# Attention with 16 heads in a conformer block: where two partial softmax sums are exchanged, values reordered once through DRAM, transposes issued in pairs

## The chip, the cores and the metric

The kernel runs on one core of a Trainium2 chip. A core has a matrix engine (PE), three engines for elementwise work (VectorE or DVE, ScalarE or ACT, GpSimd or POOL) and SyncE (SP), whose queue issues most DMA transfers. Each engine works through its own instructions in order. Times are microseconds of one execution of the whole program. The kernel before takes 1745.57 us, the median of three runs from 1742.99 to 1748.04.

## The reference

One block over a sequence of 1024 tokens of width 1024, in f32. One projection feeds a gated convolution branch, the queries, keys and values of 16 heads of 64, and two gates. Attention of a head is a mixture of three dilated windows, each a softmax of its own, mixed by their log-sums; that is one softmax over the union of the keys with counts. Then the branches are merged through the gates and a gated feed-forward layer with a short convolution follows.

```python
DILATION_GROUPS = ((128, 1), (512, 4), (2048, 16))
z = h @ w_in
glu_in, q, k, v, gate_logits = split(z)
...
for window, dilation in DILATION_GROUPS:
    o_g, lse_g = dilated_window_attention(q, k, v, slopes, window, dilation)
mix = softmax(stack(lses), axis=0)
o = einsum('gbsh,gbshd->bshd', mix, stack(outs))
...
x = x + (g_a * y_a + g_b * y_b) @ w_out
x = x + ffn(rms_norm(x))
```

## The kernel before

Every f32 operand of a product is held as two parts, high and low, so that PE works in its fast f32 form; `split` (lines 87 and 88) makes them, the high part as a rounded copy, the low part as a subtraction on DVE or POOL. The stages by time in the profile: the gated linear unit and first gates up to 235 us; the projection to q, k and v up to 519.5; attention up to 910; the merge and the output projection up to 1130; the feed-forward layer to the end.

**The projection** runs over six blocks of 512 columns: block `ch` is of kind `ch % 3` (0 q, 1 k, 2 v) and of head group `ch // 3` (heads 0 to 7, 8 to 15). So blocks 0, 1, 2 are q, k, v of group 0, and 3, 4, 5 those of group 1. Within a block there are eight token tiles of 128. The weights come in four pieces of 512 KB each (`raw_qkv`, line 92), used first by the first tile. Results are normalised and transposed three tiles later (q and k: `qh`, `ql`, two buffers each) or only split (v), and then spilled to DRAM by SP (`spill`, line 154): `dq`, `dk`, and `dv` (512 KB per tile: 128 tokens x 8 heads x 128 values, the 128 being 64 high and 64 low).

**Attention** runs over heads, each in eight slots of 128 queries. The keys of a query fall in two sets: near ones (its own and the previous tile of 128) and those of the same class modulo 4. The near scores are computed for queries in natural order, the others for queries in order of their class (`order` makes that copy on POOL). So for each head there are 8 near rows-tiles and 8 class tiles with their own minima and sums, `st[:, 0]`, and to join both into one softmax each order needs the other's numbers. They go through DRAM: `exchange` (lines 825 to 831) writes both halves, 8 KB each, out to `dst` (lines 828 and 829), reads them back in the other order into `st[:, 1]` (830 and 831). All four are on SP, so the reads stand in its queue until the writes have landed, and what follows on SP stands behind them. `factor_first` (836, 837 on DVE, then an exponential on ACT in 838) and `factor_last` (843 to 846) make a factor per query row, `share` (856, POOL) multiplies the rows with it, `flip` (865, PE) transposes a slot's tiles of 128 into PSUM (`pp`), `split` makes `ph` on ACT and `pl` on DVE, and `weigh` (880, PE) adds them times the values into `o`.

The values must lie with the keys on the partitions, in both orders. `values` (line 778 on) fetches them per head from `dv` by six transfers: four for the class-ordered tile of near keys, two for the tile of the same class. `head` fetches q, kh, kl in halves (256 KB each) and the mask.

Order: in attention the instructions of ACT, DVE and PE keep the order in which the code is written; SP and POOL are ordered by a scheduler. One loop runs over slots `at`. Slot `n` of head `h` scores; in slot 0 `exchange` of the head before; in slot `MERGE` its factors; `BACK` delays the shares, transposes and weighing of the head before; `FILL` is the rate at which matmuls of other stages (gates and the convolution's output, `next(gates)`) are put in between:

```python
if n == 2 and h + 1 < H: tiles[h + 1] = head(h + 1)
if n == 5 and h + 1 < H: order(h + 1, 0)
if n == 0 and 0 < h <= H: exchange(h - 1)
if n == 5 and h < H: values(h)
first = n == MERGE and 0 < h <= H      # MERGE = 3
s0 = at - 7 - BACK                     # shares, BACK = 5
s1 = at - 8 - BACK                     # transposes, weighed a slot later
```

Of the kernel before, what the change touches and what calls it, by code (L numbers as in the profile page):

```python
# [21 lines left out]
P = 128  # L22
D = 1024
T = 1024
# [10 lines left out]
FILL = (2.8, 1.53, 2.0)  # L35
MERGE = 3
BACK = 5
# [23 lines left out]
def block_kernel(ctx: ExitStack, tc: tile.TileContext, x, xT, w_first, g1, g2, pack, mask,  # L61
# [100 lines left out]
    dv = [dr.tile([T, 8, P], F32R, name=f"dv{i}") for i in range(2)]  # L162
# [433 lines left out]
    with tc.tile_pool(name="ph1", bufs=1, reuse_waits="tile") as p1, ExitStack() as rest:  # L596
# [137 lines left out]

        tails = []
# [39 lines left out]
    with tc.tile_pool(name="ph2", bufs=1, reuse_waits="tile") as p2:  # L775
        vals, stats, rows, factors = {}, {}, {}, {}

        def values(h):
            near, same = (p2.tile([P, 8, P], F32R, tag=f"v{i}", bufs=2, name=f"v{i}_{h}") for i in range(2))
            src = dv[h // 8]  # L780
            for r in range(4):
                fetch(near[32 * r : 32 * r + 32], src.rearrange("(i j r) h e -> r j i h e", i=8, r=4)[r][:, :, h % 8, :])
            for b in range(2):
                fetch(same[:, 4 * b : 4 * b + 4, :],
                      src.rearrange("(b p r) h e -> b p r h e", b=2, r=4)[b][:, :, h % 8, :])
# [38 lines left out]
        def exchange(h):  # L824
            st = stats[h]
            far = lambda i: dstat[i][h].rearrange("(r j) (a f) -> (j a) r f", r=4, a=4)
            own = lambda i: st[:, i, 8:16, :].rearrange("p (r b) s -> p r (b s)", r=4)
            sp.dma_start(dstat[0][h], st[:, 0, 0:8, :])
            sp.dma_start(far(1), own(0))
            sp.dma_start(own(1), far(0))  # L830
            sp.dma_start(st[:, 1, 0:8, :], dstat[1][h])
# [9 lines left out]
        def factor_last(h, w):  # L841
# [7 lines left out]
        SHARES = [[(0, 0), (1, 0), (1, 4), (0, 1)], *([(1, i), (1, 4 + i), (0, 1 + i)] for i in (1, 2, 3)),  # L849
                  [(0, 5)], [(0, 6)], [(0, 7)]]  # L850
# [75 lines left out]
        with tc.manual_schedule(engines={ENG.Activation, ENG.DVE, ENG.PE}):  # L926
            pend = []
            for at in range(8 * H + 8 + BACK + 1):
# [17 lines left out]
                if s0 >= 0 and s0 % 8 < 7 and s0 // 8 < H:  # L946
# [622 lines left out]
```

## Time and profile before

| | |
|---|---|
| median of three runs | 1745.57 us |
| profiled execution, its own time | 1747.96 us |
| span of that execution, first to last instruction | 1746.1 us |
| mean granted clock of PE | 0.991 |
| PE busy in the span | 98% |
| DMA, mean over the span | 169 GB/s, 294.36 MB |

A line of the timeline reads: start, duration, engine, source line, operation, tiles written <- tiles read, partitions x elements, and in brackets the idle time ahead with what released it. A row of the waits has the time in all, the number and the longest. In a table of stretches each row is a stretch from A to B, with the busy time of each engine in it. The granted clock is the share of its full speed that PE was allowed. `SPq` is SP's queue, on which a transfer is issued; the landing is later. "Share" of DMA is the mean busy share of the core's 16 DMA engines.

### The profile page before, as it was taken

The page shows a single profiled execution, that of the slowest core. Times are in us where ns is not written, and L with a number is a line of the kernel's source. Part 1 is how long each engine was busy: PE and PEld are TensorE (multiplying, and loading weights), DVE is VectorE, ACT ScalarE, POOL GpSimd, SP SyncE. Part 2 cuts the span into 40 slices and gives each one's busy share as a digit, 9 for nine tenths or more (in the row PEclk, how much of TensorE's full clock was granted, in tenths as well). Part 3 has the DMA queues.
Part 4 walks back from the last instruction along what each step waited for, and adds up shares of the span by engine and source line. Part 5 has one row for each costly group of instructions (what it writes and reads, how often), then busy time and mean ns, then how long its engine had stood idle before and what let it go on. Part 6 is the DMA issues. An engine that isn't in the chain of part 4 may idle for free.

```text
span 1746.1 us, 23765 instructions
## 1 busy us (share of the span) xinstructions
PE 1709.8 (98%) x8384; PEld 1427.8 (82%) x8384; DVE 1272.5 (73%) x1926; ACT 838.6 (48%) x1482; POOL 517.3 (30%) x511
## 2 busy tenths in 40 slices
PE   9999999999998999989999999999999999999999
PEld 8888888887887788878888888888888888878877
DVE  6999999989743566766645564787767777879863
ACT  5543345554344566656645342555445445533431
POOL 0078749999503455665530000000000000000000
PEclk9999999999999999999999999999999999999999
DMA  8323264553468677787537585622222222499851
GB/s 318 121 98 108 77 231 139 153 179 118 128 242 218 149 196 186 213 219 189 147 114 270 196 308 208 224 98 84 85 85 74 95 85 73 150 331 326 284 175 48
DMA packets 189590, 294.36 MB, mean 169 GB/s; under 512 B 35104, under 2 KB 100896, under 8 KB 189216
## 3 DMA queue, kind: packets, MB, share of 16 engines
q1 hardware_dynamic: 187744, 289.70, 51.5%
q10 hardware_dynamic: 1728, 3.15, 0.5%
q8 instruction: 66, 1.08, 0.3%
q14 instruction: 52, 0.43, 0.1%
HBM read 212.84 MB, written 79.95 MB: 168 GB/s over the span
## 4 chain that ended last, share of the span: by engine, by line
PE 81%; DMA 11%; DVE 3%; issue 2%; ACT 1%; SPq 1%; POOL 1%; ACTq 0%; DVEq 0%; POOLq 0%
PE qkv L151 14%; PE xz L131 6%; PE xz L132 6%; PE xz L133 6%; PE wo L151 5%; PE dx L1394 5%; DMA dst<-st 5%; PE dy L1394 4%; PE glugv L355 3%; PE y L132 2%; PE y L131 2%; PE y L133 2%; PE uxz L133 2%; PE uxz L132 2%; PE uxz L131 2%; PE o L880 2%
## 5 line engine op out<-in xcount | busy, mean ns | idle before, releaser
L636 DVE SCALAR_TENSOR_TENSOR work<-apad,pk,work 128x1024 f32<-128x1024 f32 x188 | 241.5, 1284 | 3.4
L88 DVE TENSOR_TENSOR pl<-pp,ph 128x512 fp32r<-128x512 f32 (+2 forms) x128 | 77.7, 607 | 96.6 <-ACT ph L87 96.1
L856 POOL TENSOR_SCALAR p<-p,w 128x256 f32<-128x256 f32 (+1 forms) x256 | 111.6, 458 | 54.2 <-DVE w L846 41.5
L822 ACT ACTIVATE p<-p,st 128x256 f32<-128x256 f32 (+1 forms) x256 | 118.6, 466 | 16.9 <-DVE st L815 14.9
L151 PE MATMUL qkv<-hi_qkv,hT 128*128 128x512 f32 x384 | 115.0, 393 | 0.0
L1297 DVE SCALAR_TENSOR_TENSOR u<-u,pk 128x1023 f32<-128x1023 f32 x88 | 112.2, 1277 | 1.0 <-ACT u L1295 0.7
L815 DVE CUSTOM_DVE_ANT_0 p<-s,m 128x256 f32<-128x256 f32 (+1 forms) x256 | 87.0, 377 | 33.3 <-PE s L809 30.3
L627 POOL TENSOR_TENSOR part<-prod,part 128x1024 f32<-128x1024 f32 x43 | 103.5, 2407 | 21.3 <-ACT prod L626 16.8
L87 ACT ACTIVATE ph<-pp 128x512 fp32r<-128x512 f32 (+2 forms) x128 | 67.6, 528 | 76.0 <-PE pp L865 67.7
L880 PE MATMUL o<-ph,v 128*128 128x128 f32 (+1 forms) x336 | 84.7, 311 | 15.7 <-ACT ph L87 15.7
L151 PEld LDWEIGHTS qkv<-hi_qkv,hT 128*128 128x128 f32 x384 | 71.4, 188 | 14.7
L88 DVE TENSOR_TENSOR lo_uv<-raw_uv,hi_uv 128x1024 fp32r<-128x1024 f32 x20 | 24.5, 1226 | 79.8 <-ACT hi_uv L87 79.8
L880 PE MATMUL o<-pl,v 128*64 128x128 f32 (+1 forms) x336 | 77.5, 247 | 2.9 <-DVE pl L88 2.5
L151 PE MATMUL wo<-hi_wo,mT 128*128 128x512 f32 x256 | 80.1, 391 | 0.0
L865 PE MATMUL pp<-ident,p 128*128 128x128 f32 x432 | 74.0, 283 | 6.2 <-POOL p L856 5.5
L865 PEld LDWEIGHTS pp<-ident,p 128*128 128x128 f32 x432 | 56.8, 145 | 27.4 <-POOL p L856 11.6
L880 PEld LDWEIGHTS o<-ph,v 128*128 128x128 f32 x336 | 63.1, 198 | 18.3 <-ACT ph L87 18.3
L793 POOL CAST q<-q 128x512 fp32r<-128x512 f32 x32 | 36.0, 1128 | 132.1 <-DMA q<-dq 105.2
L131 PE MATMUL xz<-blk_t,hi_s3g 128*128 128x512 f32 x176 | 68.6, 390 | 0.7 <-ACT xc L1271 0.7
L131 PE MATMUL xz<-h2left,hi_uv 128*128 128x512 f32 x176 | 68.7, 390 | 0.0
L133 PE MATMUL xz<-h2left,lo_uv 128*128 128x512 f32 x176 | 68.5, 389 | 0.0
L132 PE MATMUL xz<-blk_t,hi_s3g 128*128 128x512 f32 x176 | 68.5, 389 | 0.0
(399 smaller groups left out, 5317.2 us busy)
## 6 DMA issues: line engine op xcount, KB each, us to landing
wr<-w_down SPq DMA_DIRECT2D x45, 512.0 KB, 5.6
gr<-dff SPq DMA_DIRECT2D x62, 256.0 KB, 5.1
raw_qkv<-w_qkv SPq DMA_DIRECT2D x24, 512.0 KB, 4.3
dff<-u SPq DMA_DIRECT2D x22, 512.0 KB, 2.6
raw_uv<-w_up SPq DMA_DIRECT2D x21, 512.0 KB, 3.2
raw_ug<-w_up SPq DMA_DIRECT2D x20, 512.0 KB, 3.2
q<-dq SPq DMA_DIRECT2D x32, 256.0 KB, 5.9
dv<-v SPq DMA_DIRECT2D x16, 512.0 KB, 2.8
```

The lines of the kernel that those rows point to most:

```text
L131: pe.matmul(o, wh[:, k, :], bh[:, k, :], start=(start and k == 0), stop=False, skip_group_check=not start)
L132: pe.matmul(o, wh[:, k, :], bl[:, k, :], start=False, stop=False, skip_group_check=not start)
L133: end = pe.matmul(o, wl[:, k, :], bh[:, k, :], start=False, stop=(k == 3), skip_group_check=not start)
L151: pe.matmul(ps, l, r[:, k % 2, :], start=(n == 1), stop=(n == 3 * KT))
L627: pool.tensor_tensor(out=a[:, CW - 1 :] if j == CW - 1 else part, in0=prods[j % 3], in1=part, op=ALU.add)
L636: dve.scalar_tensor_tensor(out=a[:, CW - 1 :] if j == CW - 1 else work, in0=a[:, j : j + T], scalar=w(c, j), in1=part if j == n else work, ...
L822: act.activation(pt, pt, AF.Exp, bias=st[:, 0, at, 0:1], scale=-1.0, accum_out=st[:, 0, at, 1:2])
L856: pool.tensor_scalar(pt, pt, f, 1.0, op0=ALU.mult, op1=ALU.mult)
L865: pe.transpose(o.rearrange("p (a j) -> p j a", a=4) if j < 2 - x else o, t, ident)
L880: pe.matmul(view(o[:m]), v[:, :m], t, start=(start and i == 0), stop=(stop and i == 0), skip_group_check=True)
L1297: dve.scalar_tensor_tensor(out=acc[:, d:], in0=src[:, : T - d], scalar=w(2 - d), in1=acc[:, d:], op0=ALU.mult, op1=ALU.add)
L1394: pe.matmul(banks[n], a[:, c], b[:, d], start=(start and i == 0 and m == 0), stop=(stop and i == nf - 1 and m == 2), skip_group_check=True)
```

## The change

What it does, part by part:

- Each group of values has three DRAM tiles: `dv[g][2]` takes the spill in natural order, and `sort_values(g, tt)` copies each 512 KB tile twice, from DRAM to DRAM, into `dv[g][0]` (the near order, sorted by class within 128 tokens) and `dv[g][1]` (the class order). For group 0 this stands behind each spill in block 2; for group 1 two tiles per head behind the exchange of heads 0 to 3, that is in slot 0 of heads 1 to 4.
- `values` fetches two contiguous-row tiles with two transfers instead of six, in slot 0 of the next head, behind the head's loads.
- `exchange` is split. `exchange_out` (two writes, SP) is issued in slot 0; the next head's loads, the values and the sort copies are issued after it. `exchange_in` (two reads) is on ACT's queue in slot `MERGE - 2 = 2`.
- `MERGE` goes from 3 to 4 and `BACK` from 5 to 7; `FILL` goes down slightly; `order(h + 1, 0)` stands in slot 6 instead of 5; the shares are laid out over eight slots.
- The transposes of two slots stand together in every second slot, and `weigh` of one slot is done in each slot ahead of them.

```diff
-FILL = (2.8, 1.53, 2.0)
-MERGE = 3
-BACK = 5
+FILL = (2.7, 1.48, 2.0)
+MERGE = 4
+BACK = 7
...
-    dv = [dr.tile([T, 8, P], F32R, name=f"dv{i}") for i in range(2)]
+    dv = [[dr.tile([T, 8, P], F32R, name=f"dv{i}_{a}") for a in range(3)] for i in range(2)]
...
-                spill(dv[g8][tt * P : (tt + 1) * P], vt.rearrange("p h s d -> p h (s d)"))
+                spill(dv[g8][2][tt * P : (tt + 1) * P], vt.rearrange("p h s d -> p h (s d)"))
+                if g8:
+                    to_sort.append((g8, tt))
+                else:
+                    sort_values(g8, tt)
...
+        def sort_values(g8, tt, by=sp):
+            src = dv[g8][2].rearrange("(i j r) h e -> i r j (h e)", i=8, r=4)[tt]
+            near = dv[g8][0].rearrange("(i r j) h e -> i r j (h e)", i=8, r=4)[tt]
+            same = dv[g8][1].rearrange("(b r a j) h e -> b a r j (h e)", b=2, r=4, a=4)[tt // 4, tt % 4]
+            for dst in (near, same):
+                by.dma_start(dst.bitcast(F32), src.bitcast(F32))
...
-            src = dv[h // 8]
-            for r in range(4):
-                fetch(near[32 * r : 32 * r + 32], src.rearrange("(i j r) h e -> r j i h e", i=8, r=4)[r][:, :, h % 8, :])
-            for b in range(2):
-                fetch(same[:, 4 * b : 4 * b + 4, :],
-                      src.rearrange("(b p r) h e -> b p r h e", b=2, r=4)[b][:, :, h % 8, :])
+            for t, src in zip((near, same), dv[h // 8]):
+                fetch(t, src.rearrange("(i p) h e -> p i h e", p=P)[:, :, h % 8, :])
...
-        def exchange(h):
+        def exchange_out(h):
...
             sp.dma_start(dstat[0][h], st[:, 0, 0:8, :])
-            sp.dma_start(far(1), own(0))
-            sp.dma_start(own(1), far(0))
-            sp.dma_start(st[:, 1, 0:8, :], dstat[1][h])
+            return sp.dma_start(far(h, 1), turned(st, 0))
+
+        def exchange_in(h):
+            st = stats[h]
+            act.dma_start(turned(st, 1), far(h, 0))
+            act.dma_start(st[:, 1, 0:8, :], dstat[1][h])
...
-                    if n == 2 and h + 1 < H:
-                        tiles[h + 1] = head(h + 1)
+                    if n == 0 and h == 0:
+                        tiles[1] = head(1)
...
-                    if n == 5 and h + 1 < H:
+                    if n == 6 and h + 1 < H:
                         order(h + 1, 0)
                 if n == 0 and 0 < h <= H:
-                    exchange(h - 1)
-                if n == 5 and h < H:
-                    values(h)
-                s0 = at - 7 - BACK
+                    with tc.issue_after(exchange_out(h - 1).ins):
+                        if h + 1 < H:
+                            tiles[h + 1] = head(h + 1)
+                        values(h - 1)
+                        for t in to_sort[2 * h - 2 : 2 * h]:
+                            sort_values(*t)
+                if n == MERGE - 2 and 0 < h <= H:
+                    exchange_in(h - 1)
+                s0 = at - 6 - BACK
...
-                flips = []
                 s1 = at - 8 - BACK
-                if 0 <= s1 < 8 * H:
-                    flips.append(flip(s1 // 8, s1 % 8))
-                for w in pend:
-                    done = weigh(*w) or done
-                pend = flips
+                if pend and s1 >= 1:
+                    done = weigh(*pend.pop(0))
+                if 0 <= s1 < 8 * H and s1 % 2 == 0:
+                    pend += [flip(s // 8, s % 8) for s in (s1, s1 + 1)]
```

SP's order at the end of block 2, before: the last spills of values (`dv`), the four weight pieces of block 4 (`raw_qkv`), the first spill of block 3 (`dq`).

```order
L154 DMA dv_82<-v_6_2798 128x1024
L92 DMA raw_qkv_0_3177<-w_qkv 128x1024
L154 DMA dv_82<-v_7_2827 128x1024
L92 DMA raw_qkv_1_3183<-w_qkv 128x1024
L92 DMA raw_qkv_2_3189<-w_qkv 128x1024
L92 DMA raw_qkv_3_3195<-w_qkv 128x1024
L154 DMA dq_0_76<-qh_0_2999 512x1x128
```

The same place after the change:

```order
L154 DMA dv_2_84<-v_6_2814 128x1024
L746 DMA dv_0_82<-dv_2_84 128x1x1024
L746 DMA dv_1_83<-dv_2_84 4x32x1024
L92 DMA raw_qkv_0_3197<-w_qkv 128x1024
L154 DMA dv_2_84<-v_7_2845 128x1024
L746 DMA dv_0_82<-dv_2_84 128x1x1024
L746 DMA dv_1_83<-dv_2_84 4x32x1024
L92 DMA raw_qkv_1_3203<-w_qkv 128x1024
L92 DMA raw_qkv_2_3209<-w_qkv 128x1024
L746 DMA dv_0_82<-dv_2_84 128x1x1024
L746 DMA dv_1_83<-dv_2_84 4x32x1024
L92 DMA raw_qkv_3_3215<-w_qkv 128x1024
```

Two copies (`L746`) per tile of values now stand between the spills and the weight pieces; the last piece stands behind all sixteen copies of group 0. The shape shown is the destination's; the source of both copies is the same, 4x32x1024 (four classes of 32 rows).

SP's order around the first exchange, before (`st` is the table of minima and sums of head 0, `q`, `kh`, `kl` the loads of head 2):

```order
L157 DMA q_4517<-dq_0_74 64x1024
L157 DMA kh_4518<-dk_0_78 64x1024
L828 DMA dst_0_84<-st_4270 128x16
L829 DMA dst_0_100<-st_4270 128x4x4
L157 DMA kl_4519<-dk_1_79 64x1024
L830 DMA st_4270<-dst_0_84 128x4x4
L831 DMA st_4270<-dst_0_100 128x16
L157 DMA q_4517<-dq_1_75 64x1024
```

And after the change:

```order
L838 DMA dst_0_88<-st_4301 128x16
L839 DMA dst_0_104<-st_4301 128x4x4
L157 DMA q_4486<-dq_0_74 64x1024
...
L736 DMA m_4489<-mask 128x512
L157 DMA v_0_4497<-dv_0_82 128x8x128
L157 DMA v_0_4498<-dv_1_83 128x8x128
L746 DMA dv_0_85<-dv_2_87 128x1x1024
L746 DMA dv_1_86<-dv_2_87 4x32x1024
L746 DMA dv_0_85<-dv_2_87 128x1x1024
L746 DMA dv_1_86<-dv_2_87 4x32x1024
L240 DMA dgate_128<-gs_1_4516 128x512
```

The writes of the exchange stand ahead of the loads, and the reads are gone from SP. ACT has them, two slots on, among the exponentials (`L831`) of head 1:

```order
L831 ACTIVATE p_1_1_4526,st_4474<-p_1_1_4526,st_4474 128x128
L843 DMA st_4301<-dst_0_88 128x4x4
L844 DMA st_4301<-dst_0_104 128x16
L831 ACTIVATE p_1_2_4551,st_4474<-p_1_2_4551,st_4474 128x256
L831 ACTIVATE p_1_2_4553,st_4474<-p_1_2_4553,st_4474 128x128
```

The exponentials of head 1's later slots stand behind the reads there.

More of the change, by code (lines that the diff above doesn't have):

```diff
@@ L822, in powers @@
             act.activation(pt, pt, AF.Exp, bias=st[:, 0, at, 0:1], scale=-1.0, accum_out=st[:, 0, at, 1:2])
-        def exchange(h):
+        far = lambda h, i: dstat[i][h].rearrange("(r j) (a f) -> (j a) r f", r=4, a=4)
+        turned = lambda st, i: st[:, i, 8:16, :].rearrange("p (r b) s -> p r (b s)", r=4)
+        def exchange_out(h):
             st = stats[h]
-            far = lambda i: dstat[i][h].rearrange("(r j) (a f) -> (j a) r f", r=4, a=4)
-            own = lambda i: st[:, i, 8:16, :].rearrange("p (r b) s -> p r (b s)", r=4)
             sp.dma_start(dstat[0][h], st[:, 0, 0:8, :])
-            sp.dma_start(far(1), own(0))
-            sp.dma_start(own(1), far(0))
-            sp.dma_start(st[:, 1, 0:8, :], dstat[1][h])
+            return sp.dma_start(far(h, 1), turned(st, 0))
[3 more added lines that the diff above has]
+            act.dma_start(st[:, 1, 0:8, :], dstat[1][h])
         def factor_first(h):
@@ L847, in factor_last @@
             factors[h] = w
-        SHARES = [[(0, 0), (1, 0), (1, 4), (0, 1)], *([(1, i), (1, 4 + i), (0, 1 + i)] for i in (1, 2, 3)),
-                  [(0, 5)], [(0, 6)], [(0, 7)]]
+        SHARES = [[(0, 0), (1, 0), (1, 4), (0, 1)], [(1, 1), (1, 5), (0, 2)], [(1, 2), (1, 6), (0, 3)],
+                  [(1, 3), (1, 7), (0, 4)], [(0, 5)], [(0, 6)], [(0, 7)], []]
         def share(h, i, n):
@@ L938, in block_kernel @@
                         order(h, 1)
[L939 removed]
+                    if n == 6 and h + 1 < H:
                         order(h + 1, 0)
                 if n == 0 and 0 < h <= H:
[L942 to L946 removed]
+                    with tc.issue_after(exchange_out(h - 1).ins):
[7 more added lines that the diff above has]
+                s0 = at - 6 - BACK
+                if 0 <= s0 < 8 * H:
                     for i, k in SHARES[s0 % 8]:
```

1 line of the change is left out of this document (added).

## The prediction

> **What bounds the kernel now.** I read the page's first part, then a table of stretches, then the waits, and last the chain with one stall in full.
>
> ```profile
> PE 1709.8 (98%) x8384; PEld 1427.8 (82%) x8384; DVE 1272.5 (73%) x1926; ACT 838.6 (48%) x1482; POOL 517.3 (30%) x511
> ...
> L151 PE MATMUL qkv<-hi_qkv,hT 128*128 128x512 f32 x384 | 115.0, 393 | 0.0
> ```
>
> The matrix engine (PE) is busy for 1709.8 of 1746.1 us. The change adds and removes no matmul and no transpose, so all that it can win is PE's 36 us of idle time and what PE loses to a lowered clock; all that it can lose is new idle time. The table of stretches says where both lie. Its columns are the stretch, its length, then busy time (and instructions) of PE, PE's weight loads, VectorE (DVE), ScalarE (ACT) and GpSimd (POOL), the granted clock, the DMA share and GB/s. The first row is the loading at the start, the second block 2 of the projection (the first value block) with most of block 3, the third the rest of the projection, and the last two are attention.
>
> ```profile
> 10.00:14.00 4.00, 4.00 (x18) 3.07 (x17) 3.04 (x4) 4.00 (x7) 0.00 (x0) 1.00 1.03 420
> 348.00:425.00 77.00, 75.25 (x344) 62.02 (x343) 71.22 (x72) 42.34 (x50) 72.18 (x33) 1.00 0.39 130
> 425.00:520.00 95.00, 95.00 (x454) 78.86 (x453) 65.66 (x78) 35.55 (x50) 35.49 (x20) 1.00 0.55 189
> 520.00:640.00 120.00, 111.51 (x671) 96.02 (x670) 59.45 (x237) 65.76 (x214) 51.13 (x84) 0.94 0.76 195
> 640.00:912.00 272.00, 255.65 (x1698) 221.83 (x1696) 165.65 (x580) 163.48 (x508) 149.38 (x246) 0.97 0.66 177
> ```
>
> In attention PE is idle for 8.5 us (120 less 111.51) and 16.4 us (272 less 255.65), 24.9 us together. The clock of 0.94 and 0.97 costs up to another 7.2 and 8.2 us (6% of 120, 3% of 272). In the projection PE has nothing to win: 75.25 of 77 us busy, then 95.00 of 95. Those 95 us are the last two of its six blocks, 47.5 us a block and 5.9 for each of the eight tiles of a block. The waits within attention (time in all, times, longest) say who holds PE up there:
>
> ```profile
> DVE w L836 <- DMA st<-dst: 28.9, 13, 4.7
> ACT w L838 <- DVE w L837: 47.9, 16, 5.2
> PE o L880 <- ACT ph L87: 15.7, 10, 3.5
> SPq L830 <- DMA dst<-st: 56.0, 15, 4.9
> PE pp L865 <- POOL p L856: 5.5, 4, 4.7
> ```
>
> DVE waits 28.9 us for the exchanged sums, 13 times in 16 heads. SyncE (SP), whose queue issues the transfers in order, itself stands 56.0 us for the outgoing write before it may issue the read. ACT stands behind it, and PE waits 15.7 us for the split of the transposes that ACT makes next. One of these stalls in the timeline (start, duration, engine, line, tiles), with the stretch of normal clock gone behind it:
>
> ```profile
> 744.90 0.55 SPq L828 DMA_DIRECT2D dst<-st  x1
> 751.77 0.38 SPq L830 DMA_DIRECT2D st<-dst  x1
> 755.57 0.82 DVE L836 TENSOR_TENSOR w<-st 128x16 f32<-128x16 f32 x1 [3.35 <-DMA st<-dst]
> 757.26 0.48 ACT L87 ACTIVATE ph<-pp 128x384 fp32r<-128x384 f32 x1
> 757.80 0.46 PE L880 MATMUL o<-ph,v 128*128 128x128 f32 x1 [3.48 <-ACT ph L87]
> 759.09 0.63 PE L123 MATMUL ya<-aT,hi_co 128*128 128x512 f32 x1
> ```
>
> The outgoing write is issued at 744.90, the read back at 751.77, DVE starts at 755.57 after 3.35 us of waiting, PE at 757.80 after 3.48. The gap is followed by a matmul of 0.63 us for 512 columns (the projection's row above has 393 ns for as many). So the attention stage is bounded by PE with an exchange of 8 KB that comes some 3 us late per head.
>
> **Part 1: the exchange, the pairs, the order of the slots.** The outgoing writes go ahead of the next head's loads, the read goes on ACT's queue two slots later, the factors are made one slot later, the transposes two slots later. In the chain the outgoing writes of successive heads read so:
>
> ```profile
> 548.71 5.47 DMA dst<-st
> 571.01 5.70 DMA dst<-st
> 637.32 6.39 DMA dst<-st
> 744.90 6.81 DMA dst<-st
> 752.25 3.24 DMA st<-dst
> ```
>
> Between 548.71 and 637.32 lie four heads: 22.15 us a head, 2.77 a slot. The moves give one slot for the factors (2.77), two for the transposes (5.54), and about 3.6 us of the write's 6.81 if it lands like the read (3.24) once no load stands ahead of it: near 12 us of room against a lateness of 3.5. So the stalls of the exchange go wherever the queue isn't otherwise fuller. For 640 to 912 that is at most 16.4 + 8.2 = 24.6 us. I take **-20**, since a few of these gaps are not of the exchange (PE's 15.7 us waiting for ACT is over the whole of attention, of 24.9 idle). The ends are -24.6 and 0, the latter if the wait only moves. Pairing the transposes removes no instruction and I cost it at nothing: PE works through gate matmuls meanwhile. If that cover fails, the price is PE's wait for POOL's scaled rows, 5.5 us over all of attention in the row above. Fetching the values with two issues instead of six moves the same 512-byte pieces; it frees SP of four issues a head, which were off PE's path. The wait that SP sheds (56.0 us, 15 times, 3.7 each) is now on ACT, and what stands behind it there are the exponentials of the running head, for which DVE, POOL and then PE wait. It is two slots behind the write, 5.5 us, so it is short if the write lands like the read.
>
> **Part 2: the sort copies.** New are 32 copies of 512 KB from DRAM to DRAM (line 746 of the changed kernel), 16 per group. The trace of before has no such operation. The bounds of one: all sixteen DMA engines at the 420 GB/s of the first row (share 1.03), 0.524 MB in **1.25 us**; or a single engine at a sixteenth of that, **20 us**. Where between them depends on how many engines one copy occupies. The order of instructions shows what is different: every transfer of before starts with a count of 32, 64, 128 or 512, every copy has a side that reads 4x32x1024, four runs of rows lying apart. I take four engines, one for each run: 105 GB/s, **5.0 us**, which is also the middle of the two ends by ratio. While it runs, those four engines serve nothing queued later, and a transfer that uses all sixteen ends when its share on the four does.
>
> The Trainium skill, DMA: Bandwidth & Descriptors, section "Why a DMA increments its semaphore by 16 and not by 1", states that a DMA uses the largest number of engines up to 16 that divides the slowest dimension above 1 of both its patterns. By it a copy with 4 outermost runs has four engines and the sum below stays as it is; without it, with sixteen engines, the sum would be that of the first rival. No run here shows it yet.
>
> *Projection.* Copies of group 0 stand behind each spill of block 2 on SP, and ahead of the weights of block 4 and of the first spills of block 3:
>
> ```profile
> 348.21 2.12 SPq L154 DMA_DIRECT2D dv<-v  x2
> 382.27 7.42 SPq L92 DMA_DIRECT2D raw_qkv<-w_qkv  x3
> 402.38 0.56 SPq L154 DMA_DIRECT2D dq<-qh  x1
> 377.69 1.04 ACT L87 ACTIVATE hi_qkv<-raw_qkv 128x1024 fp32r<-128x1024 f32 x1
> 424.39 1.41 PE L151 MATMUL qkv<-hi_qkv,hT 128*128 128x512 f32 x5
> ```
>
> From 348 on the four engines have the work of before, 0.39 of 77 us = 30 us, less about 5 for spills of block 3 that stand behind the weights, and 16 x 5.0 = 80 us of copies: the fourth weight piece lands at 348 + 25 + 80 = 453, and ACT's split of it ends at 454. PE starts block 4 at 424.39 and needs that piece some three quarters of a tile of 5.9 us later, 428.8. The first spill of block 3, issued at 402.38 before, is queued behind too; with two buffers the third tile's q waits for it, and PE's accumulators fill up at about the same time. PE stalls for 454 less 428.8, **+25**. Ends: +3 if nothing of the old work is in the way (348 + 2.8 for the first spill + 80), +73 if a copy takes 8 us; and no cost at 1.25 us, where 20 us of copies fit into the 0.61 that is free.
>
> *Attention.* Group 1 is copied in heads 1 to 4, two tiles (four copies, 20 us) per head. The old work on each engine there is 0.76 x 22.15 = 16.8 us a head, together 36.8 against 22.15. Four heads: 147 less 88.6 = 58.7 us late, of which the room of 12 us from part 1 is taken once: **+47**. Ends: +20, if the 0.76 holds waiting and only 195 of 420 GB/s is work (0.46 x 88.6 + 80 - 88.6 - 12); +94 for copies of 8 us. The exchange, the next head's loads and the values all stand in this queue. In these heads the stalls of before are inside the new ones, so part 1 wins nothing there.
>
> **Sum.** -20 + 25 + 47 = +52. The profiled execution took 1747.96 us (span 1746.1 and 1.9 around it); that gives 1800. The median of the runs, 1745.57, is 2.4 below it, so 1798 there; I say **1799**.
>
> **The rivals.**
>
> *Sixteen engines for a copy (faster).* The mechanism is the same queue with the price of 1.25 us: then 20 us of copies fit beside the projection's 0.39 and raise the 0.76 of heads 1 to 4 to 0.76 + 5/22.15 = 0.99, just within. All stalls of the exchange go, three quarters of the 24.9 + 15.4 us: -30, 1716. The point from which it decides is a copy of about 1.4 us in attention, and three to four us in the projection. For it speaks that every transfer of before reaches all engines; against it that none of those has so short a first count. Chance 0.13.
>
> *The wait only moves.* ACT's read lands no sooner than SP's, since both queues share the engines. Part 1 wins nothing: 25 + 47 = +72, 1818. Against it: the room of 12 us. Chance 0.06.
>
> *A copy costs 8 us,* because it reads and writes the same memory: 73 + 94 - 20 = +147, 1893; 20 us on one engine goes far beyond. Chance 0.06.
>
> *Only one stage pays,* since SP's own waits keep the copies from piling up, or the weights come early enough: 25 - 20 or 47 - 20, 1751 to 1773. Chance 0.11; a fifth of it within 0.3%.
>
> *The forecast:* 0.64.
>
> **How the numbers follow.** A measurement of this kernel can tell about 0.3% (5 us) from no change. Faster by more is the first rival alone, 0.13. Within 0.3%: 0.02 from the fourth. Slower: 0.85. The range reaches from 1755, where the fourth rival's larger half and the forecast's low ends lie (both low at once, 3 + 20 - 20, would be 1749), to 1880, just under the 8 us copies. It leaves out the first rival, about 0.05 above and a little below, some 0.2.
>
> **What would show it.** Right: a stretch from about 400 to 455 in which the DMA share falls toward 0.25 at some 100 GB/s, with PE idle for 20 to 30 us of it before block 4's first tile is through; copies that land long after 5 us because they queue for one another; head periods over 30 us for heads 1 to 5 and at or under 21.5 us later; from head 6 on no wait of DVE for st<-dst and a clock near 1.00. Wrong: PE at 95 us of 95 in the projection and periods of 22 us from the first head (then the copies are spread), or the wait of DVE for the exchange still there in late heads (then part 1 is wrong), or a bound that I do not name, such as ACT held by its own DMA's wait.

## The result and the profile after

The changed kernel takes 1837.12 us (median of 4 runs, 1828.01 to 1839.97) against 1744.99 for the kernel before (four runs as well): a ratio of 1.0517, 95% interval 1.0477 to 1.0557. It is slower by 5%, inside the range of 1755 to 1880 and well above the 1799 forecast. The profiled execution took 1839.97 us with a span of 1837.7.

The page's first part and the same kinds of stretches as before, with the borders moved to where the stages now lie (columns as before; the first two are the blocks with copies and the wait for block 4, the last two attention, first with copies, then mostly without):

```profile
PE 1722.9 (94%) x8384; PEld 1439.7 (78%) x8384; DVE 1270.6 (69%) x1926; ACT 837.3 (46%) x1482; POOL 516.7 (28%) x511
```

```profile
348.00:425.00 77.00, 67.61 (x286) 54.75 (x285) 59.17 (x58) 35.43 (x41) 61.36 (x28) 0.93 0.43 161
425.00:480.00 55.00, 36.18 (x151) 28.51 (x150) 29.87 (x33) 12.81 (x18) 22.72 (x12) 0.78 0.55 177
...
570.00:700.00 130.00, 88.21 (x520) 75.22 (x519) 44.15 (x187) 50.95 (x169) 39.73 (x65) 0.83 0.66 172
700.00:1010.00 310.00, 273.93 (x1799) 240.21 (x1799) 177.48 (x614) 174.62 (x540) 160.19 (x266) 0.95 0.68 177
```

PE did the same 8384 matmuls. It now idles for 9.4 us in the first row and 18.8 in the second, where it had idled for 1.75 and nothing, and the clock granted there fell to 0.93 and 0.78. Attention begins at the first row below instead of the second (first score of head 0, after and before the change), and the merge's first operand is made at 1006.51 instead of 911.27:

```profile
556.58 0.22 PE L814 MATMUL s<-kh,q 128*128 128x128 f32 x1
1006.51 3.91 ACT L87 ACTIVATE oT<-raw_o 128x1024 fp32r<-128x1024 f32 x4 [0.53 <-ACT ya L254]
```

```profile
519.55 0.22 PE L805 MATMUL s<-kh,q 128*128 128x128 f32 x1
911.27 2.01 ACT L87 ACTIVATE oT<-raw_o 128x1024 fp32r<-128x1024 f32 x2 [0.54 <-ACT ya L254]
```

So the projection lost 37.0 us, attention 58.2 (449.93 against 391.72), and 3.6 came back later.

**The copies.** The DMA view of the stretch from 348 to 460 us shows, in 40 slices of 2.8 us, the busy tenths of the 16 engines and the rate:

```profile
DMA  1883234482285226222622295224932283427290
GB/s 69 326 249 124 111 126 152 164 320 113 99 266 225 105 105 244 101 105 105 252 105 105 105 256 236 105 105 140 341 121 105 107 276 144 176 105 241 82 280 5
```

Many slices stand at 105 GB/s with a busy share of two tenths, a quarter of 420 GB/s on a quarter of the engines. The longest stall in the projection, by the waits from 425 to 480 us and PE's timeline:

```profile
ACT qh L694 <- DMA dq<-qh: 25.8, 1, 25.8
DVE ql L695 <- ACT qh L694: 24.5, 1, 24.5
...
454.37 1.12 PE L689 MATMUL qt<-ident,qn 128*128 128x128 f32 x4 [16.88 <-DVE ql L695]
```

The holder that ended last was the spill of q, not the fourth weight piece: the two `qh` buffers were full, ACT stood 25.8 us for a spill that queued behind the copies, and PE stood 16.88 us behind DVE and ACT. In attention a spill of a gate does the same (first head with copies; SP, ACT and PE in the timeline):

```profile
589.74 7.68 SPq L746 DMA_DIRECT2D dv<-dv  x4
597.52 5.78 SPq L240 DMA_DIRECT2D dgate<-gs  x2
616.38 0.69 ACT L239 ACTIVATE gs<-gate,pk 128x512 f32<-128x512 f32 x1 [17.53 <-DMA dgate<-gs]
617.61 0.47 PE L893 MATMUL o<-ph,v 128*128 128x128 f32 x1 [15.55 <-ACT ph L87]
```

256 KB issued at 597.52 behind four copies lets ACT go on at 616.38, after 17.53 us; ACT's split of the transposes stands behind it, and PE waits 15.55.

Three times after that ACT is held by something else, its own read of the sums. The read can't be issued until the write has landed, the write is behind the copies, and the exponentials stand behind the read on ACT. The last of the three stalls, in ACT's and PE's timelines, and the waits of ACT's exponentials from 557 to 1002 us:

```profile
732.22 0.51 ACT L831 ACTIVATE p<-p,st 128x256 f32<-128x256 f32 x1 [16.68 <-issue]
733.63 0.47 PE L893 MATMUL o<-ph,v 128*128 128x128 f32 x1 [13.51 <-ACT ph L87]
...
ACT p L831 <- issue: 32.7, 3, 16.7
ACT p L831 <- DMA dst<-st: 13.6, 1, 13.6
```

ACT's reads are issued at 659.60, 694.12 and 730.97, and PE goes on after 11.63, 10.55 and 13.51 us of waiting. With the 15.55 of the gate's spill these are PE's four long stalls of attention, 51.2 us together.

**The exchange.** The chain of waits has these transfers of the sums (start, time to landing): the write of head 2, then the reads of heads 6 and 13.

```profile
644.46 15.06 DMA dst<-st
771.64 8.55 DMA st<-dst
929.93 10.45 DMA st<-dst
```

While copies run, the write takes 13 to 15 us (heads 2 to 4). That of head 2 lands at 659.52, and ACT issues its read at 659.60. Later, with no copies left, the read takes 8.5 to 10.5 us on ACT's queue, where it took 1.9 (median) on SP's before. The waits of attention (557 to 1002 us):

```profile
PE o L893 <- ACT ph L87: 68.5, 17, 15.6
DVE w L849 <- DMA st<-dst: 27.5, 13, 3.3
```

DVE waits 27.5 us, 13 times, against 28.9 and 13 before. So part 1 won nothing, and PE's waits for ACT grew from 15.7 to 68.5, of which 51.2 are the four long stalls.

### The profile page after: what moved, and what is told of

It reads as the page before. It is cut to its first block, busy times and chain, and to the rows that moved or that the text cites. A ratio compares the mean times of both kernels' runs of the same rounds, so it can differ in the third digit from the quotient of the medians.

```text
span 1837.7 us, 23719 instructions
## 1 busy us (share of the span) xinstructions
PE 1722.9 (94%) x8384; PEld 1439.7 (78%) x8384; DVE 1270.6 (69%) x1926; ACT 837.3 (46%) x1482; POOL 516.7 (28%) x511
## 4 chain that ended last, share of the span: by engine, by line
PE 79%; DMA 13%; DVE 2%; ACT 2%; issue 2%; POOL 1%; SPq 0%; ACTq 0%; DVEq 0%; POOLq 0%
PE qkv L151 10%; PE dx L1410 7%; PE xz L131 5%; PE xz L133 5%; PE xz L132 5%; DMA st<-dst 5%; PE dy L1410 5%; PE wo L151 5%; PE glugv L355 2%; DMA dst<-st 2%; PE o L893 2%; PE y L133 2%; PE y L132 2%; PE y L131 2%; PE uxz L131 2%; PE uxz L132 2%
## 5 line engine op out<-in xcount | busy, mean ns | idle before, releaser
L88 DVE TENSOR_TENSOR pl<-pp,ph 128x512 fp32r<-128x512 f32 (+2 forms) x128 | 71.9, 603 | 137.7 <-ACT ph L87 137.6
L831 ACT ACTIVATE p<-p,st 128x256 f32<-128x256 f32 (+1 forms) x256 | 119.1, 468 | 69.4 <-issue 32.7
L893 PE MATMUL o<-ph,v 128*128 128x128 f32 (+1 forms) x336 | 77.5, 286 | 68.5 <-ACT ph L87 68.5
L151 PE MATMUL qkv<-hi_qkv,hT 128*128 128x512 f32 x384 | 122.0, 413 | 8.2 <-ACT hi_qkv L87 4.8
L151 PEld LDWEIGHTS qkv<-hi_qkv,hT 128*128 128x128 f32 x384 | 75.8, 200 | 25.5 <-ACT hi_qkv L87 5.6
L87 ACT ACTIVATE ph<-pp 128x512 fp32r<-128x512 f32 (+2 forms) x128 | 61.1, 528 | 67.2 <-PE pp L878 66.5
L151 PE MATMUL qkv<-lo_qkv,hT 128*128 128x512 f32 x192 | 69.3, 397 | 0.0
L131 PE MATMUL xz<-h2left,hi_uv 128*128 128x512 f32 x176 | 68.6, 390 | 0.0
L133 PE MATMUL xz<-h2left,lo_uv 128*128 128x512 f32 x176 | 68.5, 389 | 0.0
L132 PE MATMUL xz<-blk_t,hi_s3g 128*128 128x512 f32 x176 | 68.5, 389 | 0.0
L132 PE MATMUL xz<-h2left,hi_uv 128*128 128x512 f32 x176 | 68.5, 389 | 0.0
```

Of the source, the lines that this page charges most:

```text
L88: by.tensor_tensor(out=lo, in0=src, in1=hi.bitcast(F32), op=ALU.subtract)
L131: pe.matmul(o, wh[:, k, :], bh[:, k, :], start=(start and k == 0), stop=False, skip_group_check=not start)
L132: pe.matmul(o, wh[:, k, :], bl[:, k, :], start=False, stop=False, skip_group_check=not start)
L133: end = pe.matmul(o, wl[:, k, :], bh[:, k, :], start=False, stop=(k == 3), skip_group_check=not start)
L151: pe.matmul(ps, l, r[:, k % 2, :], start=(n == 1), stop=(n == 3 * KT))
L831: act.activation(pt, pt, AF.Exp, bias=st[:, 0, at, 0:1], scale=-1.0, accum_out=st[:, 0, at, 1:2])
```

## The experiments

All ratios are to the kernel before, run on the same chip beside each.

### Where the loss is: the shape of the copies

**e1_spread.** The copies' rows in the other order, so that 32 and not four stand outermost:

```diff
-            src = dv[g8][2].rearrange("(i j r) h e -> i r j (h e)", i=8, r=4)[tt]
-            near = dv[g8][0].rearrange("(i r j) h e -> i r j (h e)", i=8, r=4)[tt]
-            same = dv[g8][1].rearrange("(b r a j) h e -> b a r j (h e)", b=2, r=4, a=4)[tt // 4, tt % 4]
+            src = dv[g8][2].rearrange("(i j r) h e -> i j r (h e)", i=8, r=4)[tt]
+            near = dv[g8][0].rearrange("(i r j) h e -> i j r (h e)", i=8, r=4)[tt]
+            same = dv[g8][1].rearrange("(b r a j) h e -> b a j r (h e)", b=2, r=4, a=4)[tt // 4, tt % 4]
```

> The change with the sort copies' dimensions in the other order, 32 runs of rows outermost where it had four classes; the same bytes and the same places. Engines (a copy holds four DMA engines for 5 us because four is its outermost count): it takes 1.25 us now, PE's stall in blocks 3 and 4 of the projection goes (-37 us) and heads 2 to 5 take about 22 us instead of 34 to 38 (-55): 1745 us, about the time before the change. Volume (33 MB more read and written, and 32 more instructions in SP's queue, are what costs): 1815 us or more.

Measured: 1750.74 us, 1.0049 (1.0033 to 1.0066). By the ratios 82 us are gone with the order of two dimensions; the bytes and the instructions are the same. From 348 to 420 us of its trace:

```profile
DMA  5799899999999999999999998000002240440350
GB/s 243 289 244 248 282 421 414 371 319 414 421 398 403 410 401 405 348 341 335 407 389 412 355 401 348 39 0 0 0 0 74 72 145 0 146 146 0 119 172 12
```

All sixteen engines at up to 421 GB/s, and the queue is empty at 394 us.

**e4_two.** Each copy as two, two classes outermost in each:

```diff
             for dst in (near, same):
-                by.dma_start(dst.bitcast(F32), src.bitcast(F32))
+                for a in (0, 2):
+                    by.dma_start(dst[a : a + 2].bitcast(F32), src[a : a + 2].bitcast(F32))
```

> Each sort copy as two, with two classes of rows outermost. Engines: two engines hold 0.5 MB for 10 us. In the projection 348 + 25 + 160 = 533 against 429, +104; heads 1 to 4 cost 16.8 + 40 us each, 227 less 88.6 less 12 = +127: about 1976 us, with slices at 52 GB/s in the profile. Volume: as the changed kernel, 1837, plus a few us for 32 more issues.

Measured: 1991.67 us (1.1428, 1.1402 to 1.1455), two runs, 16 above what the engines' theory gives. The rate from 360 to 560 us:

```profile
GB/s 54 52 52 52 174 136 169 52 52 52 52 53 52 272 109 52 48 53 56 52 53 52 260 212 57 52 52 145 52 52 52 184 105 118 123 95 100 292 320 76
```

52 GB/s with two outermost runs, 105 with four, 421 with 32 on all sixteen engines: a sixteenth of 420 for each engine in use. Volume, the rival, falls. The rule of the Trainium skill that the prediction cites (DMA: Bandwidth & Descriptors, section "Why a DMA increments its semaphore by 16 and not by 1") gives two, four and sixteen engines for 2, 4 and 32 outermost runs. The traces agree with it by these three rates.

**e3_group0_four.** The short outermost dimension for group 0 alone:

```diff
+            if g8:
+                src = dv[g8][2].rearrange("(i j r) h e -> i j r (h e)", i=8, r=4)[tt]
...
+            else:
+                src = dv[g8][2].rearrange("(i j r) h e -> i r j (h e)", i=8, r=4)[tt]
...
```

> As e1_spread for group 1 alone; group 0's copies in the projection still have four runs outermost. Engines: the projection loses its 37 us as in the changed kernel, attention nothing, 1782 us. Volume: above 1815. If the two stages share one loss (a late start that attention makes good): below 1770.

Measured: 1788.22 us, 1.0256 (1.0234 to 1.0279). In ratios times 1743: the copies cost 36 us in the projection (1.0256 less 1.0049), and the rest of the loss, 45, is what they cost in attention (1.0517 less 1.0256). Attention does not make good what the projection loses. The profiles give 37.0 for the projection of the changed kernel, and 50.2 for attention: from the first score to the merge's first operand 449.93 us there and 399.69 here (553.92 to 953.61).

### Where the gain of part 1 went

**e2_no_sort.** No copies, the six fetches of before, all else as changed:

```diff
-                if g8:
-                    to_sort.append((g8, tt))
-                else:
-                    sort_values(g8, tt)
...
-            for t, src in zip((near, same), dv[h // 8]):
-                fetch(t, src.rearrange("(i p) h e -> p i h e", p=P)[:, :, h % 8, :])
+            src = dv[h // 8][2]
+            for r in range(4):
+                fetch(near[32 * r : 32 * r + 32], src.rearrange("(i j r) h e -> r j i h e", i=8, r=4)[r][:, :, h % 8, :])
...
```

> The change without the sort copies: the values are fetched in six transfers per head out of the natural order as before, while the exchange, the slots and the pairs of transposes stay as changed. Both theories of the copies: 1745 us within 8. Theory that the exchange is worth its 20 us and the loss in late heads comes from values fetched otherwise: 1725. Theory that the exchange only moved its wait: 1745 (the read lands some 8 us after its issue on ACT's queue, as in the changed kernel).

Measured: 1748.30 us, 1.0029 (1.0014 to 1.0043): 5 us slower than before, not 20 faster. What the 5 us are is not shown. The copies at sixteen engines add 0.0020, 3 to 4 us, which the two intervals do not tell from nothing. The trace is of the fastest of ten runs, 1743.09. Landings from 640 to 912 us (queue, count, size, median), first in the kernel before:

```profile
st<-dst SPq DMA_DIRECT2D x24, 8.0 KB, 1.9
dst<-st SPq DMA_DIRECT2D x22, 8.0 KB, 6.2
```

Then in e2_no_sort, with its waits from 520 to 912 us:

```profile
dst<-st SPq DMA_DIRECT2D x22, 8.0 KB, 2.8
st<-dst ACTq DMA_DIRECT2D x22, 8.0 KB, 7.1
...
DVE w L849 <- DMA st<-dst: 23.6, 10, 4.5
PE o L893 <- ACT ph L87: 20.3, 10, 4.0
```

The write is as quick as hoped (6.2 before, 2.8 now), but the read takes 7.1 where it had taken 1.9. Together they take longer than before, 9.9 us against 8.1, and the factors stand one slot later only. The transposes' two more slots did not help: DVE and ACT stand at the factors in their own order, and PE's wait for the split behind them is 20.3 us where it was 15.7.

**e5_read_first.** Both reads on SP right behind the writes, the loads behind the reads:

```diff
-            act.dma_start(turned(st, 1), far(h, 0))
-            act.dma_start(st[:, 1, 0:8, :], dstat[1][h])
+            sp.dma_start(turned(st, 1), far(h, 0))
+            return sp.dma_start(st[:, 1, 0:8, :], dstat[1][h])
...
                     with tc.issue_after(exchange_out(h - 1).ins):
+                        back = exchange_in(h - 1)
+                    with tc.issue_after(back.ins):
...
-                if n == MERGE - 2 and 0 < h <= H:
-                    exchange_in(h - 1)
```

> e2_no_sort with both reads of the exchange on SP's queue right behind the writes, and the next head's loads and the values behind the reads. Theory that the read meets the loads (it lands 7 us after its issue because the loads issued just ahead of it fill the engines; that is where the gain of part 1 went): the read lands in 2 to 3 us, some 7 us after the head's start and ahead of slot 4 at 11, DVE no longer waits for it, and 15 to 20 us go: 1728 to 1733. Theory that the exchange was no longer what bounds (the 20 us PE still waits for ACT's split come from the pairs or from ACT's own queue): 1748 as e2_no_sort. If the loads now come too late: above 1755, with PE waiting for kh or q.

Measured: 1723.81 us, 0.9887 (0.9872 to 0.9902), the fastest kernel here together with e12_flip_first, which comes further down. The read lands in 2.1 us, DVE has no wait for it left, and PE waits 0.3 us for ACT's split:

```profile
st<-dst SPq DMA_DIRECT2D x22, 8.0 KB, 2.1
```

**e8_read_behind.** The other way, with `exchange_in` on SP as well:

```diff
                     with tc.issue_after(exchange_out(h - 1).ins):
                         if h + 1 < H:
                             tiles[h + 1] = head(h + 1)
                         values(h - 1)
...
+                        exchange_in(h - 1)
-                if n == MERGE - 2 and 0 < h <= H:
-                    exchange_in(h - 1)
```

> e2_no_sort with the reads on SP's queue behind the next head's loads and values. Theory that the read is late because the loads share its engines, whatever the queue: it lands some 10 us after its issue or later than on ACT, DVE waits longer than in e2_no_sort and the time is 1755 or more. Theory that ACT's queue is the slow one: the read takes 2 us from its issue as in the kernel before, and the time is 1740 or less.

Measured: 1828.44 us, 1.0485 (1.0464 to 1.0506), one round. The read does not take 10 us from its issue but 4.4; it is issued late, since SP issues the loads first: in one head the writes go out at 766.24 and the read at 778.23. DVE waits 85.3 us:

```profile
st<-dst SPq DMA_DIRECT2D x20, 8.0 KB, 4.4
...
DVE w L849 <- DMA st<-dst: 85.3, 13, 8.2
```

So what counts is where the read stands against the loads. Whether ACT's queue has a price of its own beside that, the last two reads of e2_no_sort tell in part. Heads 14 and 15 have no next head whose loads would stand ahead of the read, only values (issued at 856.94 and 876.85):

```profile
st<-dst ACTq DMA_DIRECT2D x1, 8.0 KB, 2.8
st<-dst ACTq DMA_DIRECT2D x1, 8.0 KB, 4.2
```

The other fourteen took 4.2 to 11.4 us. So most of the 7.1 goes with the loads and not with ACT's queue; the read was not tried there with nothing at all ahead of it. Nor was the lower `FILL` of the change tried alone.

**e7_before_merge4.** The kernel before with one slot more, for the factors and for all behind them:

```diff
-MERGE = 3
-BACK = 5
+MERGE = 4
+BACK = 6
```

> The kernel before with MERGE 4 and BACK 6 alone: the factors one slot later, exchange, loads and single transposes as before. Same theory as for e6_merge5: the read of before lands up to 4.7 us after DVE wants it, one slot is 2.8 us, so most of the 16 us that PE loses to it go: 1728 to 1735. Theory that lateness just follows (the writes land later still since more is queued): 1745.

Measured: 1729.13 us, 0.9918 (0.9903 to 0.9932). DVE's wait falls from 28.9 us to 1.5, PE's for ACT's split from 15.7 to 1.0; PE's for POOL grows from 5.5 to 13.2:

```profile
DVE w L836 <- DMA st<-dst: 1.5, 2, 1.1
PE o L880 <- ACT ph L87: 1.0, 1, 1.0
PE pp L865 <- POOL p L856: 13.2, 11, 3.0
```

**e6_merge5.** The same step on e2_no_sort, which already had MERGE 4:

```diff
-MERGE = 4
+MERGE = 5
...
-                if n == MERGE - 2 and 0 < h <= H:
+                if n == MERGE - 3 and 0 < h <= H:
...
-                s0 = at - 6 - BACK
+                s0 = at - 7 - BACK
...
-        SHARES = [[(0, 0), (1, 0), (1, 4), (0, 1)], [(1, 1), (1, 5), (0, 2)], [(1, 2), (1, 6), (0, 3)],
+        SHARES = [[(0, 0), (1, 0), (1, 4), (0, 1), (1, 1), (1, 5), (0, 2)], [(1, 2), (1, 6), (0, 3)],
```

> e2_no_sort with the factors one slot later (slot 5), the read still on ACT in slot 2, and the first shares of a head in one slot. Theory that only the slot of the factors decides, since the transposes' two slots of delay don't help a DVE and an ACT that already stand at the factors: DVE's wait for the read (23.6 us in e2_no_sort, up to 4.5 at a time) falls under 8, and the time to about 1732. Theory that the wait moves to POOL's shares, which now come just ahead of the transposes: DVE's wait falls as well but PE waits for POOL instead, 1745 or more.

Measured: 1747.55 us, 1.0023 (1.0013 to 1.0033), no better than e2_no_sort. DVE's wait fell only from 23.6 to 14.9, and POOL now waits for the factors, 50.8 us where e2_no_sort has 3.3, just ahead of the transposes:

```profile
DVE w L849 <- DMA st<-dst: 14.9, 10, 3.8
POOL p L869 <- DVE w L859: 50.8, 14, 8.3
```

The time and POOL's wait are the rival's, but PE's matmuls hardly wait for POOL (0.9 us; its weight loads 14.9, 56 times), so that rival is borne out by half. From 520 to 912 us PE is busy 8 us longer than in e2_no_sort (371.55 against 363.46) for about as many matmuls (2371 and 2378), so that it idles less and is no further on. Why they take longer, and why DVE's wait fell by so little, stays open.

**e11_before_order.** SP's order of e5_read_first put into the kernel before, MERGE 3 and BACK 5 kept:

```diff
-                    exchange(h - 1)
-                if n == 5 and h < H:
-                    values(h)
+                    with tc.issue_after(exchange(h - 1).ins):
+                        if h + 1 < H:
+                            tiles[h + 1] = head(h + 1)
+                        if h < H:
+                            values(h)
```

> The kernel before with one thing altered, SP's order at the exchange: its writes and reads ahead of the next head's loads and the values, which are issued behind them; MERGE 3, BACK 5, single transposes. Theory that the read meets the loads: it lands some 7 us after the head's start against 8.3 for slot 3, DVE's wait for it (28.9 us) falls under 6 and the time to 1727 to 1733. Theory that a slot more is needed as well: 1738 or more.

Measured: 1758.60 us, 1.0074 (1.0052 to 1.0097): slower than before, which neither theory had forecast. The time lies in the open range of the second (1738 or more), but not for its reason: the wait for the read is gone altogether, without a slot more. Instead PE waits 30.7 us for POOL's shares. One place in POOL's timeline, and that wait:

```profile
766.45 1.05 POOL L793 CAST q<-q 128x512 fp32r<-128x512 f32 x1 [7.77 <-DMA q<-dq]
768.70 2.43 POOL L856 TENSOR_SCALAR p<-p,w 128x128 f32<-128x128 f32 x6
...
PE pp L865 <- POOL p L856: 30.7, 16, 5.5
```

POOL stands 7.77 us for the q of the next head, which now is loaded behind the exchange, and the shares are queued behind that cast. The change moved the cast to slot 6 and the transposes two slots on; this kernel did neither. That these two are what e5_read_first needs was not tried one by one.

### Together, and the pairs

**e9_both.** The copies of e1_spread with the exchange of e5_read_first, both edits as shown there; the loads, the values and the copies stand behind the reads:

```diff
                     with tc.issue_after(exchange_out(h - 1).ins):
+                        back = exchange_in(h - 1)
+                    with tc.issue_after(back.ins):
...
                         for t in to_sort[2 * h - 2 : 2 * h]:
                             sort_values(*t)
```

> The whole change with two places altered: the sort copies with 32 runs outermost (as e1_spread) and the exchange's reads on SP right behind its writes, ahead of the loads (as e5_read_first). Theory that these two are all that the change lost by: 1722 to 1727, within 3 of e5_read_first, DVE without a wait for the read. If the copies' 20 us per head fill heads 1 to 4 even at sixteen engines: 1728 to 1735, with the difference in the first five heads.

Measured: 1734.82 us, 0.9949 (0.9931 to 0.9967). The second case: 11 us behind e5_read_first. Stretches of e9_both, then of e5_read_first:

```profile
520.00:640.00 120.00, 109.21 (x647) 93.72 (x645) 59.15 (x235) 66.78 (x214) 47.31 (x81) 0.94 0.84 240
640.00:912.00 272.00, 264.41 (x1782) 232.77 (x1781) 173.74 (x587) 172.08 (x521) 152.05 (x250) 0.99 0.73 203
```

```profile
520.00:640.00 120.00, 116.50 (x739) 101.41 (x737) 68.71 (x266) 73.83 (x240) 53.94 (x89) 1.00 0.81 196
640.00:912.00 272.00, 264.35 (x1728) 231.65 (x1729) 174.48 (x564) 171.71 (x502) 146.13 (x242) 0.98 0.78 205
```

From 520 to 640 PE is busy for 7.3 us less at a lower clock; from 640 on it is busy alike. The first score comes 2.1 us later (521.26 against 519.21), the sixth write of the sums 17.0 us later (662.47 against 645.47), and the later heads make up some 6 of that. So the loss lies mainly in the heads with copies, and even spread over sixteen engines the copies do not pay for the four issues they save.

**e10_single** and **e12_flip_first.** e5_read_first with the transposes one slot at a time; in the second the transposes again ahead of the products, as before the change. First e10_single, then e12_flip_first, each against e5_read_first:

```diff
                 if pend and s1 >= 1:
                     done = weigh(*pend.pop(0))
-                if 0 <= s1 < 8 * H and s1 % 2 == 0:
-                    pend += [flip(s // 8, s % 8) for s in (s1, s1 + 1)]
+                if 0 <= s1 < 8 * H:
+                    pend.append(flip(s1 // 8, s1 % 8))
```

```diff
-                if pend and s1 >= 1:
-                    done = weigh(*pend.pop(0))
-                if 0 <= s1 < 8 * H and s1 % 2 == 0:
-                    pend += [flip(s // 8, s % 8) for s in (s1, s1 + 1)]
+                if 0 <= s1 < 8 * H:
+                    pend.append(flip(s1 // 8, s1 % 8))
+                if s1 >= 1:
+                    done = weigh(*pend.pop(0))
```

> e5_read_first with the transposes of one slot at a time, each slot, as before the change; MERGE 4 and BACK 7 stay. Theory that the pairs are worth nothing: 1724 within 3. If pairs save PE's changes between transposes and products: 1730 or more. If they cost PE waits (two slots' shares must be there at once): 1720 or less.

> e10_single with one thing altered: in each slot the transposes are issued ahead of the products of the slot before, as in the kernel before the change, so that a slot's split has the transposes and the products of one more slot to hide behind. Theory that e10_single lost because its products came too soon behind the split (PE waited 18.6 us for DVE's low part and 8.4 for ACT's high part): those waits fall under 8 together and the time to 1735 or less. Theory that single transposes cost by the change of work on PE (the product that follows a transposition takes longer: 311 ns in the kernel before, 274 in e5_read_first, over 336 of them 12 us): 1735 to 1740 with few waits. If both are wrong: 1745 or more.

Measured: e10_single 1752.26 us, 1.0057 (1.0039 to 1.0075); e12_flip_first 1725.19, 0.9895 (0.9877 to 0.9913), the same as e5_read_first. Alone, e10_single reads as if pairs were worth 28 us. The waits, of e10_single and then of e12_flip_first, say what it was:

```profile
PE o L893 <- DVE pl L88: 18.6, 53, 1.7
PE o L893 <- ACT ph L87: 8.4, 10, 2.0
```

```profile
PE o L893 <- DVE pl L88: 8.6, 14, 1.6
PE o L893 <- ACT ph L87: 2.0, 2, 1.0
```

The products came too soon behind the split. With the transposes first these waits fall from 27.0 to 10.6 us, just above the 8 expected, and the pairs are worth nothing. The 16 us are most of the 27 between the two kernels; the rest does not show in these waits.

## Why the prediction was right, and where it was wrong

- **The unit of spreading, four engines and 5.0 us a copy:** right. 105 GB/s at two tenths of the engines' share, and e4_two and e1_spread at 52 and 421.
- **Projection, +25:** right mechanism, size 36 to 37. PE's new idle time is 26 us (28.2 in the first two rows of the stretches, less 1.75), as forecast. What the term lacked is the clock behind the stalls, 0.93 and 0.78 there, which the prediction had counted for the stalls of before; of 67.61 and 36.18 us busy, 7% and 22% are up to 12.7. In the records it is some 8 us: the projection's two groups of matmuls that differ take 122.0 and 69.3 us in all instead of 115.0 and 68.4, for as many. And the last holder was the spill of q, which the prediction named second, not the weight piece.
- **Attention, +47:** the queue behind the copies was right, the near hit partly luck. The runs give 45 us (e3_group0_four; 50 by the profiles). But the 47 are 58.7 less 12 for the room of part 1, and that room was not there, so that the copies themselves were forecast some 10 us too dear. The writes of the sums in the changed kernel's SP timeline stand at 579.50 for the first and 747.39 for the sixth, 33.6 us a head over five heads, four of them with copies; forecast were 36.8 for a head with copies and 22.15 for one without, 33.9 on average. Single heads don't follow it: they take 39.0, 25.9, 36.2, 35.7 and 31.1 us. Nor did the prediction have the way to PE in three of the four long stalls: it expected ACT's wait at the read to be "short if the write lands like the read", and the write took 13 to 15 us.

- **Part 1, -20:** this step failed. It put "near 12 us of room against a lateness of 3.5"; the rest of the change alone is 5 us slower than before (e2_no_sort), and DVE waits 27.5 us in the changed kernel where it had waited 28.9. Two of its three pieces were not room. The two slots for the transposes don't move the point where DVE and ACT stand (e2_no_sort: DVE still waits 23.6 us); a slot more for the factors, with all behind them, does, 14 us in e7_before_merge4. The 3.6 us that the write gained, the read lost: it met the very loads that had been put behind the write, 7.1 us for 1.9. The rival "the wait only moves" had this, with a chance of 0.06 and 1818; with the 11 us that the projection took beyond its term it would have been 1829.
- **The cover of the pairs:** right at nothing (e12_flip_first), but only in the order of transposes and products that hides the split.
- **What would show it:** the 105 GB/s, PE's stall before block 4's first tile is through, and heads over 30 us (four of five) came; heads at 21.5 us later, a clock near 1.00 and the end of DVE's wait did not, and by the prediction's own words part 1 is what that refutes. The bound that it gave as its example of one not named, ACT held by its own DMA's wait, came as well, three times.

So 1799 came out 38 us low: roughly 20 from part 1 that was not there, 5 that it cost, and some 11 in the projection, most of it the clock.

## What to carry to other kernels

The copies between DRAM tensors ran at 52, 105 and up to 421 GB/s with 2, 4 and 32 runs outermost: look at the outermost dimension first, since on a shared queue the copies on four engines held up the spills and the writes behind them. A small transfer that another engine waits for is late by what is issued between its two halves, so put nothing between the write and the read, and see that what now comes later is not missed elsewhere (e11_before_order). And a delay given to a later step is no room for an engine that has to stand, in order, at an earlier one.

## What the runs showed of the hardware that was not expected

A read of 8 KB took 1.9 us on SP's queue, which had stood still until the write landed (the kernel before), and 7.1 on ACT's queue while SP's loads were running (e2_no_sort). The stalls in the projection cost some 8 us in longer matmul records beyond their own 26, at a granted clock of 0.78 in the stretch that holds the longest. Products right behind transposes have longer records, without the kernel being slower by it; the groups of `o<-ph` (count, busy, mean ns) from 557 to 890 us in e12_flip_first, and with pairs in e5_read_first:

```profile
L893 PE MATMUL o<-ph,v 128*128 128x128 f32 (+1 forms) x336 | 82.8, 303 | 2.5 <-ACT ph L87 2.0 <-DMA v<-dv 0.3
```

```profile
L893 PE MATMUL o<-ph,v 128*128 128x128 f32 (+1 forms) x336 | 72.9, 274 | 0.4 <-ACT ph L87 0.3
```

303 ns against 274, some 10 us over 336 of them, at 1725.19 and 1723.81 us. In e10_single, with single transposes behind the products, it is 278 ns.
